# The up projection of a gated feed-forward layer, turned from channels on the partitions to positions on the partitions, with the transpose moved behind it

## The chip, the core and the metric

The kernel is one program on one core of a Trainium2 chip. The metric is the device time of one execution in microseconds (us). TensorE is called PE below, its weight loads PEld, VectorE DVE, ScalarE ACT, GpSimd POOL and SyncE SP. A matmul on PE has a stationary operand of 128 x 128 elements, which a load brings into the array, and a moving operand whose columns stream past it.

## The reference, cut to what matters

One layer: a token mixer with a convolution branch and a state-space branch, cross-attention, and then the feed-forward part, which is all that the change touches. There are 256 positions, a model width of 2048 and a hidden width of 5632. All arrays are 32-bit floats.

```
def causal_dwconv(x, w):
    """Depthwise causal conv over positions. x (B, L, C), w (K, C); output t reads t-K+1..t."""
    ...

def conv_ffn(h, w_up, dw_w, w_down):
    up = causal_dwconv(h @ w_up, dw_w)
    gate, val = jnp.split(up, 2, axis=-1)
    return (jax.nn.silu(gate) * val) @ w_down

h = rmsnorm(x, ffn_norm_g[i])
x = x + conv_ffn(h, ffn_w_up[i], ffn_dw_w[i], ffn_w_down[i])
```

So `h @ w_up` is 256 x 2048 times 2048 x 11264, the convolution has three taps along the positions (FFN_K = 3), with its own three weights for each of the 11264 channels, and the first half of the channels gates the second.

## The kernel before, in words

**Weights and slots.** All weights of the program form one stream of pieces of 128 x 1024 elements, and one piece is one *slot* of work. There are 586 slots. A DMA brings two pieces at once (`raw`, 1 MB, L207). For each piece ACT rounds the values to the matmul's 32-bit format (`hi`, L221) and DVE subtracts that from the original (`lo`, L222), so that a product is made of three terms, hi times hi, lo times hi and hi times lo. `take` asks for the pieces up to three slots ahead (`AHEAD = 3`), and four buffers each hold `hi` and `lo`. So the conversion of the piece for slot n + 3 waits until PE is done with the piece of slot n - 1.

**Two forms of a slot.** `by_token` says which of two forms a block of 512 weight columns has. Both make the same three products, on 6144 moving columns in a slot.

- The *wide* form (`mm_wide`, L250 and L253): the weights are stationary and the activations move. The result has the channels on the partitions. For each 128 x 128 tile of weights there is one matmul with 512 moving columns (the high and the low part of the activations side by side, L250), and one with 256 (L253): 8 and 8 in a slot, 16 weight loads. The results of the high and the low part stand in two halves of PSUM and are added afterwards (L277 on ACT, L278 on DVE).
- The *token* form (`tok_piece`, L300, L301, L304): the activations are stationary and the weights move, 512 columns at a time. The result has the positions on the partitions. There are 12 matmuls and 12 loads in a slot, and all three products add up in one place.

The up projection is wide. The projections before and after it that add to the residual (`w_out`, `xa_w_o`, `ffn_w_down`, and `conv_w_pw`) have the token form.

**The feed-forward stage.** `PAIRS` splits the hidden width into 11 pairs of blocks: a pair is block q of the gates (s = 0) and block 11 + q of the values (s = 1), each of 512 columns and of 8 slots. Pass 1 runs six pairs (96 slots), then the down projection over their 3072 rows (48 slots). Pass 2 runs five pairs (80 slots), then the last part of the down projection (40 slots). After each up block comes the scaling by the root mean square of its position (`rs`, a row that is the same on all partitions, L398 on DVE, into `up`, which has two columns of zeros in front), then the three taps: the first by ACT (L1226), the other two by DVE (L1208), each shifted by one position along the free axis. After block s = 1 of a pair comes the gate: Silu on ACT (L1232), the product on DVE (L1212) and the split into hi and lo for the down projection (L338, L339, into `as` or `fs`).

**Order.** Nothing is scheduled by a planner; the code's own order stands in each engine's queue. `defer(k, fn)` lays work aside until k slots later, and `pump`, at the end of each slot, lets out what is due. So the names below "end of slot k" count slots of the next block. Each engine works through its queue in order.

**Turning.** `turned` (L309) transposes a block of 256 positions x 512 channels on PE: 8 matmuls of 128 x 128 against the unit matrix (L316), into two buffers of PSUM (`aux`, four of them). It is used already where the residual becomes the next projection's activations (`resid`, and `merge` in the mixer). `rows` (L1155) turns the reciprocal root `rc`, which has the positions on the partitions, into the row `rs` by two small matmuls (L1164).

Of the kernel before, what the change touches and what calls it, by code (L numbers as in the profile page):

```python
# [8 lines left out]
F32 = mybir.dt.float32  # L9
F32R = mybir.dt.float32r  # L10
AF = mybir.ActivationFunctionType
ALU = mybir.AluOpType
# [36 lines left out]

BOTH = ((0, 0), (1, 0), (0, 1), (1, 1), (2, 0), (3, 0), (2, 1), (3, 1))  # L50
START = ((0, 0), (0, 1), (1, 0), (1, 1), (2, 0), (3, 0), (2, 1), (3, 1))
FIRST = {("w_in", 4), ("xa_w_kv", 0), ("xa_w_q", 0), ("ffn_w_up", 0)}


def by_token(w, nb):

    return w in ("ssm_w_glu", "conv_w_pw", "w_out", "xa_w_o", "ffn_w_down") or (w, nb // 4) == ("xa_w_kv", 1) or (w == "w_in" and nb > 5)


def stream():  # L60


    o = []

    def g(w, blocks, kqs):
        for nb in blocks:
            if by_token(w, nb):
                o.extend((False, w, 512 * nb, 512 * kq + 256 * h) for kq in kqs for h in range(2))
            elif (w, nb) in FIRST:
                o.extend((True, w, 512 * nb + 256 * h, 512 * kq) for kq, h in (START if w == "w_in" else BOTH))  # L70
            else:
                o.extend((True, w, 512 * nb + 256 * h, 512 * kq) for h in range(2) for kq in kqs)
    k4, k2 = range(4), range(2)
    g("w_in", (4, 5, 2, 0, 3, 1, *range(6, 14)), k4)
    g("xa_w_kv", range(8), k4)
    for b in range(4):
        g("ssm_w_glu", (4 + b, b), k2)
    g("conv_w_pw", range(4), k2)
    g("w_out", range(4), k4)
    g("xa_w_q", range(4), k4)  # L80
    g("xa_w_o", (0, 1), range(3))
    g("xa_w_o", (0, 1), (3,))
    g("xa_w_o", (2, 3), k4)
    for pairs in PAIRS:
        for q in pairs:
            g("ffn_w_up", (q, 11 + q), k4)
        g("ffn_w_down", range(4), pairs)
    assert len(o) % 2 == 0
    return o


class Body:
# [167 lines left out]
    def gemm(self, w, nb, xs, then, kqs=None, after=None):  # L260


        if by_token(w, nb):
            ps = self.mm_tile()
            for n, kq in enumerate(kqs or range(len(xs))):
                self.tok_piece(ps, w, nb, kq, xs[n], n == 0, n == len(xs) - 1)
                if after is not None:
                    after(n)
            self.defer(0, lambda: then(ps))
            return  # L270
# [11 lines left out]
        ps = [None, None]  # L282
        for m, (kq, h) in enumerate((START if w == "w_in" else BOTH) if (w, nb) in FIRST else [(kq, h) for h in range(2) for kq in range(4)]):
            if kq == 0:
# [18 lines left out]
                m = slice(mt * 128, mt * 128 + 128)  # L303
                nc.tensor.matmul(ps[:, mt, :], xh[:, kt, m], wl, start=False, stop=z)  # L304

    def turned(self, x, k, then):


        nc = self.nc  # L309

        def f():
            ps = [self.aux() for _ in range(2)]
            for j in range(4):
                for tt in range(2):
                    o = (j % 2) * 256 + tt * 128
                    nc.tensor.transpose(ps[j // 2][:, o:o + 128], x[:, tt, 128 * j:128 * j + 128], self.ident)  # L316

            def g():
                for j in range(2):
                    then(ps[j].rearrange("p (a t) -> p a t", a=2), j)  # L320
            self.defer(1, g)
        self.defer(k, f)


# [720 lines left out]
    def attend(self, A, xs, rq):  # L1045
        nc = self.nc
        v = nc.vector
# [93 lines left out]
        w = "xa_w_o"  # L1141
        pss = {}

        def outp(b, kq):
            if kq == 0:
                pss[b] = self.mm_tile()
            self.tok_piece(pss[b], w, b, kq, os_[kq], kq == 0, kq == 3)
            if kq == 3:
                self.defer(0, lambda: done(b, pss[b]))

        sq = self.xb.tile([128, 2, 4], F32, tag="sq", name=self.nm("sq"), bufs=2)
        rs, rc = self.rs_tile(), self.xb.tile([128, 2], F32, name="rc3")
        xs2 = [None] * 4

        def rows():  # L1155

            dg = self.st([128, 2, 128])
            for tt in range(2):
                v.tensor_scalar(dg[:, tt, :], self.ident, rc[:, tt:tt + 1], None, ALU.mult)

            def f():
                ps = self.aux()
                for tt in range(2):
                    nc.tensor.matmul(ps[:, tt * 128:tt * 128 + 128], self.ones, dg[:, tt, :], start=True, stop=True)  # L1164
                self.defer(1, lambda: nc.scalar.copy(rs, ps[:, 0:256]))
            self.defer(1, f)

        def done(b, ps):
            x = self.res[:, :, 512 * b:512 * b + 512]
            v.tensor_add(x, ps, x)  # L1170
            self.spare -= 1.2
            xs2[b] = self.split_tiles(self.xb, "b", b)
            self.resid(b, "ffn_g", sq, xs2[b])
            if b == 3:
                self.defer(2, lambda: self.tok_rs(sq, rc))
                self.defer(3, rows)

        def nxt(h):
            def f(n):
# [12 lines left out]
        for b in (2, 3):  # L1192
            for k in range(4):
                outp(b, k)
        return xs2, rs


    def ffn(self, F, xs, rs):
        nc = self.nc
        v = nc.vector  # L1200
        buf = [F.tile([128, 4, 258], F32, name=f"up{a}") for a in range(2)]
        for t in buf:
            nc.gpsimd.memset(t[:, :, 0:2], 0.0)

        def taps(c, u, s, q, ks):
            for k in ks:
                for tap in (1, 2):
                    v.scalar_tensor_tensor(out=c[:, k, :], in0=u[:, k, tap:tap + 256], scalar=self.par("fdw", (44 * s + 4 * q + k) * 3 + tap),  # L1208
                                           in1=c[:, k, :], op0=ALU.mult, op1=ALU.add)

        def gate(cv, hl):
            v.tensor_mul(cv[1], cv[0], cv[1])  # L1212
            self.plain_split(cv[1], *hl)

        sq = self.xb.tile([128, 2, 4], F32, tag="sq", name=self.nm("sq"), bufs=2)
        for pairs in PAIRS:
            act = [None] * len(pairs)
            for n, q in enumerate(pairs):
                cv = []

                def up(ps, s=0, n=n, q=q, cv=cv):
                    u = buf[s]
                    self.scaled(u[:, :, 2:258], ps, rs)
                    c = self.xc() if s else F.tile([128, 4, 256], F32, tag="cv", name=self.nm("cv"), bufs=2)
                    for k in range(4):
                        nc.scalar.activation(c[:, k, :], u[:, k, 0:256], AF.Copy, scale=self.par("fdw", (44 * s + 4 * q + k) * 3))  # L1226
                    self.defer(1, lambda: taps(c, u, s, q, (0, 1)), 1.6)
                    self.defer(2, lambda: taps(c, u, s, q, (2, 3)), 1.6)
                    cv.append(c)
                    if s:  # L1230
                        hl = act[n] = self.split_tiles(self.xa, "a", n) if n < 4 else self.split_tiles(F, "f", n)
                        self.defer(3, lambda: nc.scalar.activation(cv[0], cv[0], AF.Silu))  # L1232
                        self.defer(4, lambda: gate(cv, hl), 1.2)

                for s in range(2):
                    self.gemm("ffn_w_up", 11 * s + q, xs, lambda t, s=s, up=up: up(t, s))
            last = pairs[-1] == 10
            if last:
                gf = self.xb.tile([128, 2048], F32, tag="b0", name="gf", bufs=1)
                nc.sync.dma_start(out=gf, in_=self.i["fg"].partition_broadcast(128))  # L1240
            for b in range(3 if last else 4):
                def down(ps, b=b):
                    x = self.res[:, :, 512 * b:512 * b + 512]
                    v.tensor_add(x, ps, x)
                    self.spare -= 1.2
                    if last:
                        self.resid(b, None, sq, None)
                        self.defer(2, lambda: v.tensor_mul(x, x, gf[:, 512 * b:512 * b + 512].unsqueeze(1).to_broadcast([128, 2, 512])), 1.1)
                self.gemm("ffn_w_down", b, act, down, list(pairs))
        self.finish(sq, gf, act, list(PAIRS[1]))  # L1250
# [160 lines left out]
```

## Time and profile before

| | |
|---|---|
| median of 3 runs | 1709.28 us (1708.51 to 1709.82) |
| the profiled execution | 1709.71 us, its span 1707.9 us |
| PE busy | 1691.1 us, 99% of the span |
| PEld, DVE, ACT busy | 84%, 72%, 52% |
| granted PE clock, mean | 0.998 |
| up projection, pass 1 | 964.48 to 1235.77 us |
| down projection, pass 1 | 1235.77 to 1366.33 us |
| up projection, pass 2 | 1366.33 to 1591.33 us |

The stages' bounds are the starts of their first matmuls. A row of a group of instructions reads: line, engine, operation, output <- inputs, shapes, count, then busy us and the mean ns of one, then idle time before it and what ended it. A row of the chain of waits reads: start us, duration us, what. A matmul's duration holds its pipelined end too, so the time that one costs is read from one start to the next, not from its duration.

### The profile page before, as it was taken

The numbers are of one execution on the slowest core, as the hardware profiler recorded it, in microseconds if no ns is written. First come the engines' busy times: TensorE is split into PE (matmuls) and PEld (weight loads), VectorE is DVE, ScalarE is ACT, GpSimd is POOL, SyncE is SP. The second block draws the span as 40 slices with busy tenths as digits, with TensorE's granted clock in tenths as the row PEclk, the third lists the DMA queues.
The fourth block names the chain that finished last, engine by engine and source line by source line (L and its number), as shares of the span: only waits on it lengthen the run. The fifth ranks groups of instructions, "written<-read, shape, count | busy, mean of one in ns | idle before, by whom it ended". The sixth has DMA issues, their size and how long they took to land.

```text
span 1707.9 us, 22702 instructions
## 1 busy us (share of the span) xinstructions
PE 1691.1 (99%) x8868; PEld 1438.1 (84%) x8868; DVE 1231.5 (72%) x1627; ACT 895.6 (52%) x1200; POOL 4.3 (0%) x14
## 2 busy tenths in 40 slices
PE   7999999999999999999999999999999999999998
PEld 6888888888888888888988888888888888888886
DVE  6879999899999766556565567777764467777754
ACT  6565665765545644455454555554543345555543
POOL 0000000000000000000000000000000000000000
PEclk9999999999999999999999999999999999999999
DMA  7745555765566565655544544555555555555653
GB/s 284 248 178 179 204 203 196 259 237 196 187 231 218 196 255 209 222 186 209 197 161 172 187 171 186 198 197 181 189 197 197 190 182 183 186 179 191 225 195 122
DMA packets 61643, 340.85 MB, mean 200 GB/s; under 512 B 7904, under 2 KB 16224, under 8 KB 24160
## 3 DMA queue, kind: packets, MB, share of 16 engines
q1 hardware_dynamic: 61536, 339.41, 55.7%
q8 instruction: 69, 1.13, 0.3%
q14 instruction: 38, 0.31, 0.1%
HBM read 326.66 MB, written 12.58 MB: 199 GB/s over the span
## 4 chain that ended last, share of the span: by engine, by line
PE 98%; DMA 1%; DVE 0%; ACT 0%; issue 0%; SPq 0%; DVEq 0%; ACTq 0%
PE mm L250 31%; PE mm L253 16%; PE mm L300 15%; PE mm L301 15%; PE mm L304 15%; DMA raw<-in_ws_dram 1%; PE aux L316 1%; PE aux L1263 1%; PE aux L1262 1%; PE aux L1261 1%; PE aux L638 1%; PE aux L685 0%; PE aux L584 0%; PE aux L1083 0%; PE aux L1082 0%; PE aux L1081 0%
## 5 line engine op out<-in xcount | busy, mean ns | idle before, releaser
L222 DVE TENSOR_TENSOR lo<-raw,hi 128x1024 fp32r<-128x1024 f32 (+1 forms) x586 | 708.7, 1218 | 428.3 <-ACT hi L221 427.9
L221 ACT CAST hi<-raw 128x1024 fp32r<-128x1024 f32 (+1 forms) x586 | 608.4, 1048 | 657.0 <-PE mm L301 335.9
L250 PE MATMUL mm<-bs,hi 128*128 128x512 f32 x1664 | 522.7, 395 | 0.0
L253 PEld LDWEIGHTS mm<-bs,lo 128*128 128x128 f32 x1664 | 312.3, 188 | 75.9
L300 PE MATMUL mm<-hi,as 128*128 128x512 f32 x864 | 338.6, 392 | 0.0
L301 PE MATMUL mm<-hi,as 128*128 128x512 f32 x864 | 336.4, 389 | 0.0
L253 PE MATMUL mm<-bs,lo 128*128 128x256 f32 x1664 | 331.6, 281 | 0.0
L304 PE MATMUL mm<-lo,as 128*128 128x512 f32 x864 | 266.2, 389 | 0.0
L250 PEld LDWEIGHTS mm<-bs,hi 128*128 128x128 f32 x1664 | 256.2, 188 | 0.2
L250 PE MATMUL mm<-as,hi 128*128 128x512 f32 x640 | 203.3, 399 | 8.3 <-ACT hi L221 7.5
L300 PEld LDWEIGHTS mm<-hi,as 128*128 128x128 f32 x864 | 162.2, 188 | 34.1 <-issue 0.7
L304 PEld LDWEIGHTS mm<-lo,as 128*128 128x128 f32 x864 | 162.2, 188 | 34.0
L301 PEld LDWEIGHTS mm<-hi,as 128*128 128x128 f32 x864 | 162.3, 188 | 32.7
L253 PEld LDWEIGHTS mm<-as,lo 128*128 128x128 f32 x640 | 120.5, 189 | 30.4 <-DVE lo L222 2.3
L253 PE MATMUL mm<-as,lo 128*128 128x256 f32 x640 | 126.6, 279 | 1.0 <-DVE lo L222 1.0
L250 PEld LDWEIGHTS mm<-as,hi 128*128 128x128 f32 x640 | 98.0, 190 | 9.7 <-ACT hi L221 7.8
L751 DVE SCALAR_TENSOR_TENSOR co<-h,prm,co 128x256 f32<-128x256 f32 x240 | 100.9, 478 | 0.0
L278 DVE TENSOR_TENSOR st<-mm,st 128x512 f32<-128x512 f32 x72 | 49.2, 684 | 9.0 <-ACT st L277 9.0
L300 PE MATMUL mm<-hi,gs 128*128 128x512 f32 x128 | 50.7, 396 | 0.0
L301 PE MATMUL mm<-hi,gs 128*128 128x512 f32 x128 | 50.7, 396 | 0.0
L277 ACT COPY st<-mm 128x512 f32<-128x512 f32 x72 | 41.6, 578 | 0.1
L1208 DVE SCALAR_TENSOR_TENSOR xc<-up,prm,xc 128x256 f32<-128x256 f32 x88 | 40.6, 482 | 1.6
(281 smaller groups left out, 1295.9 us busy)
## 6 DMA issues: line engine op xcount, KB each, us to landing
raw<-in_ws_dram SPq DMA_DIRECT2D x291, 1024.0 KB, 4.8
gd<-st SPq DMA_DIRECT2D x8, 512.0 KB, 6.4
st<-gd SPq DMA_DIRECT2D x8, 512.0 KB, 5.7
xc<-in_mem_dram SPq DMA_DIRECT2D x4, 512.0 KB, 7.2
kd<-st SPq DMA_DIRECT2D x4, 512.0 KB, 4.3
vd<-st SPq DMA_DIRECT2D x4, 512.0 KB, 7.0
res<-in_xt_dram SPq DMA_DIRECT2D x4, 512.0 KB, 5.8
xc<-kd SPq DMA_DIRECT2D x4, 512.0 KB, 5.7
```

What stands on the lines that cost most here:

```text
L221: nc.scalar.copy(hi[:, k], src[:, k])
L222: nc.vector.tensor_sub(lo[:, k], src[:, k], hi[:, k].bitcast(F32))
L250: nc.tensor.matmul(ps[:, ct, :], hi[:, kt, ct * 128:ct * 128 + 128], x.t[:, :, kt, :], start=a, stop=False, skip_group_check=True)
L253: nc.tensor.matmul(ps[:, ct, 0:256], lo[:, kt, ct * 128:ct * 128 + 128], x[0][:, kt, :], start=False, stop=z, skip_group_check=True)
L277: self.nc.scalar.copy(o, ps[:, :, 256:512])
L278: self.nc.vector.tensor_add(o, ps[:, :, 0:256], o)
L300: nc.tensor.matmul(ps[:, mt, :], xh[:, kt, m], wh, start=a, stop=False)
L301: nc.tensor.matmul(ps[:, mt, :], xl[:, kt, m], wh, start=False, stop=False)
L304: nc.tensor.matmul(ps[:, mt, :], xh[:, kt, m], wl, start=False, stop=z)
L316: nc.tensor.transpose(ps[j // 2][:, o:o + 128], x[:, tt, 128 * j:128 * j + 128], self.ident)
L751: v.scalar_tensor_tensor(out=o, in0=self.h[:, k, j:j + 256], scalar=w, in1=o, op0=ALU.mult, op1=ALU.add)
L1208: v.scalar_tensor_tensor(out=c[:, k, :], in0=u[:, k, tap:tap + 256], scalar=self.par("fdw", (44 * s + 4 * q + k) * 3 + tap), in1=c[:, k, : ...
```

## The change

`ffn_w_up` goes into the token form. Its result now stands in one PSUM tile with the positions on the partitions, where the scaling is one number for each partition: ACT scales it out of PSUM into `u` by `rc` (two instructions, L1198 of the changed kernel). `turned` transposes `u` on PE one slot later. The taps read the transposed block where it lies, in PSUM: ACT makes the tap of the same position for two channel tiles (L1204), DVE adds the other two (L1209), now with outputs that start one or two positions later in place of the zero columns. A new argument of `turned`, `apart`, lets out the second half of the block one slot after the first. The gate comes after five slots in place of four. The buffers `up`, their clearing, `rows` and the row `rs` of this stage fall away, and so do the addition of the two PSUM halves and the interleaved order of the first up block (`FIRST`).

```
-FIRST = {("w_in", 4), ("xa_w_kv", 0), ("xa_w_q", 0), ("ffn_w_up", 0)}
+FIRST = {("w_in", 4), ("xa_w_kv", 0), ("xa_w_q", 0)}
...
-    return w in ("ssm_w_glu", "conv_w_pw", "w_out", "xa_w_o", "ffn_w_down") or ...
-    return w in ("ssm_w_glu", "conv_w_pw", "w_out", "xa_w_o", "ffn_w_down") or (w, nb // 4) == ("xa_w_kv", 1) or (w == "w_in" and nb > 5)
+    return w in ("ssm_w_glu", "conv_w_pw", "w_out", "xa_w_o", "ffn_w_up", "ffn_w_down") or (w, nb // 4) == ("xa_w_kv", 1) or (w == "w_in" and nb > 5)
...
-    def turned(self, x, k, then):
+    def turned(self, x, k, then, apart=0):
...
-            def g():
-                for j in range(2):
-                    then(ps[j].rearrange("p (a t) -> p a t", a=2), j)
-            self.defer(1, g)
+            for j in range(2):
+                self.defer(1 + j * apart, lambda j=j: then(ps[j].rearrange("p (a t) -> p a t", a=2), j))
         self.defer(k, f)
...
-        def rows():
-            dg = self.st([128, 2, 128])
...
-                self.defer(3, rows)
...
-        return xs2, rs
+        return xs2, rc
...
-    def ffn(self, F, xs, rs):
+    def ffn(self, F, xs, rc):
...
                 def up(ps, s=0, n=n, q=q, cv=cv):
-                    u = buf[s]
-                    self.scaled(u[:, :, 2:258], ps, rs)
+                    u = F.tile([128, 2, 512], F32, tag="u", name=self.nm("u"), bufs=2)
+                    for tt in range(2):
+                        nc.scalar.activation(u[:, tt, :], ps[:, tt, :], AF.Copy, scale=rc[:, tt:tt + 1])
                     c = self.xc() if s else F.tile([128, 4, 256], F32, tag="cv", name=self.nm("cv"), bufs=2)
-                    for k in range(4):
-                        nc.scalar.activation(c[:, k, :], u[:, k, 0:256], AF.Copy, scale=self.par("fdw", (44 * s + 4 * q + k) * 3))
-                    self.defer(1, lambda: taps(c, u, s, q, (0, 1)), 1.6)
-                    self.defer(2, lambda: taps(c, u, s, q, (2, 3)), 1.6)
+
+                    def taps(p, j):
+                        w = lambda k, tap: self.par("fdw", (44 * s + 4 * q + k) * 3 + tap)
+                        for a in range(2):
+                            nc.scalar.activation(c[:, 2 * j + a, :], p[:, a, :], AF.Copy, scale=w(2 * j + a, 2))
+                        for a in range(2):
+                            k = 2 * j + a
+                            for tap in (1, 0):
+                                d = 2 - tap
+                                v.scalar_tensor_tensor(out=c[:, k, d:256], in0=p[:, a, 0:256 - d], scalar=w(k, tap), in1=c[:, k, d:256],
+                                                       op0=ALU.mult, op1=ALU.add)
+                        self.spare -= 1.9
+                    self.turned(u, 1, taps, 1)
                     cv.append(c)
...
-                        self.defer(4, lambda: gate(cv, hl), 1.2)
+                        self.defer(5, lambda: gate(cv, hl), 1.2)
```

On PE, in the first up block before the change (`mm_8209` and `mm_8267` are its two halves, `bs` the activations, `aux_8344` the row `rs`):

```order
L253 MATMUL mm_8209<-bs_8058,lo_8235 128x256 x2
L1164 MATMUL aux_8344<-st_8321,cst 128x128 x2
L250 MATMUL mm_8209<-bs_8231,hi_8268 128x512 x2
L253 MATMUL mm_8209<-bs_8231,lo_8269 128x256 x2
...
L250 MATMUL mm_8267<-bs_8058,hi_8301 128x512 x2
L253 MATMUL mm_8267<-bs_8058,lo_8302 128x256 x2
```

And on PE after the change, between the second and the third slot of the second up block (`mm_8367`), where the first block's `u_8384` is turned into two buffers of PSUM:

```order
L301 MATMUL mm_8367<-hi_8333,bs_7839 128x512
L304 MATMUL mm_8367<-lo_8334,bs_7839 128x512 x2
L316 MATMUL aux_8406<-cst,u_8384 128x128 x4
L316 MATMUL aux_8407<-cst,u_8384 128x128 x4
L300 MATMUL mm_8367<-hi_8351,bs_7897 128x512
L301 MATMUL mm_8367<-hi_8351,bs_7897 128x512
```

The small matmuls of the row are gone, the slots have changed their form, and 8 transposes stand behind the second slot of each following block.

On ACT, from the end of the first up block on, before the change (`st_8390` takes the low half of the first block out of PSUM, `cv_8439` is its tap):

```order
L277 COPY st_8390<-mm_8209 128x512
L221 CAST hi_8395<-raw_8299 128x1024
L221 CAST hi_8416<-raw_8299 128x1024
L277 COPY st_8390<-mm_8267 128x512
L1226 ACTIVATE cv_8439<-up_8204,prm 128x256 x4
L221 CAST hi_8446<-raw_8347 128x1024
L221 CAST hi_8470<-raw_8347 128x1024
```

And after it:

```order
L221 CAST hi_8368<-raw_8281 128x1024
L1198 ACTIVATE u_8384<-mm_8204,rc_6502 128x512 x2
L221 CAST hi_8390<-raw_8315 128x1024
L221 CAST hi_8416<-raw_8315 128x1024
L1204 ACTIVATE cv_8387<-aux_8406,prm 128x256 x2
L221 CAST hi_8440<-raw_8349 128x1024
L1204 ACTIVATE cv_8387<-aux_8407,prm 128x256 x2
```

The two copies out of PSUM have become two scalings, one behind the other, and the four first taps come two and three slots later, two at a time, each behind the conversion of a weight piece.

More of the change, by code (lines that the diff above doesn't have):

```diff
@@ L1151, in attend @@
         sq = self.xb.tile([128, 2, 4], F32, tag="sq", name=self.nm("sq"), bufs=2)
-        rs, rc = self.rs_tile(), self.xb.tile([128, 2], F32, name="rc3")
+        rc = self.xb.tile([128, 2], F32, name="rc3")
         xs2 = [None] * 4
-        def rows():
-            dg = self.st([128, 2, 128])
[L1158 to L1166, printed above, removed]
         def done(b, ps):
@@ L1194, in attend @@
                 outp(b, k)
-        return xs2, rs
-    def ffn(self, F, xs, rs):
+        return xs2, rc
+    def ffn(self, F, xs, rc):
         nc = self.nc
         v = nc.vector
[L1201 to L1209, printed above, removed]
         def gate(cv, hl):
```

## The prediction

> **What bounds the kernel now.** I read the page first: span, busy shares, granted clock, and the chain of work that ended last.
>
> ```profile
> span 1707.9 us, 22702 instructions
> PE 1691.1 (99%) x8868; PEld 1438.1 (84%) x8868; DVE 1231.5 (72%) x1627; ACT 895.6 (52%) x1200; POOL 4.3 (0%) x14
> PEclk9999999999999999999999999999999999999999
> PE 98%; DMA 1%; DVE 0%; ACT 0%; issue 0%; SPq 0%; DVEq 0%; ACTq 0%
> ```
>
> The chain is PE from end to end. A busy row alone would not prove that, since a matmul's row holds its pipelined end, so next I read who made PE wait, in the whole program:
>
> ```profile
> PE mm L250 <- ACT hi L221: 7.5, 2, 6.4
> PE mm L253 <- DVE lo L222: 1.0, 2, 0.5
> PE mm L250 <- DVE as L333: 0.7, 1, 0.7
> ```
>
> That is 9.2 us, in the mixer's first stage by the operands' names (`as` from x). In the feed-forward stage PE waits for nobody. So the time of that stage is the sum of the intervals between PE's starts, and what ACT and DVE win is worth nothing as long as they stay ahead. The question is therefore how many us of PE the change takes away and adds. I take that from the stages, by the timeline of PE at their bounds and the busy time of each engine in the windows between them (window, length, then PE, PEld, DVE, ACT, POOL, clock, DMA share, GB/s):
>
> ```profile
> 964.48 0.63 PE L250 MATMUL mm<-bs,hi 128*128 128x512 f32 x2
> ...
> 1235.77 0.39 PE L300 MATMUL mm<-hi,as 128*128 128x512 f32 x1
> ...
> 1366.33 0.63 PE L250 MATMUL mm<-bs,hi 128*128 128x512 f32 x2
> ...
> 1591.33 0.39 PE L300 MATMUL mm<-hi,as 128*128 128x512 f32 x1
> ```
>
> ```profile
> 1366.33:1591.33 225.00, 225.00 (x1282) 195.87 (x1281) 158.75 (x189) 113.46 (x144) 0.00 (x0) 1.00 0.52 187
> 1235.77:1366.33 130.56, 130.56 (x578) 108.15 (x577) 69.37 (x63) 54.51 (x56) 0.00 (x0) 1.00 0.54 193
> 964.48:1235.77 271.29, 271.29 (x1549) 236.33 (x1548) 194.00 (x237) 142.57 (x186) 0.00 (x0) 1.00 0.52 187
> 696.00:742.00 46.00, 46.00 (x212) 38.26 (x212) 25.32 (x27) 22.54 (x34) 0.00 (x0) 1.00 0.58 211
> ```
>
> Pass 2 of the up projection is 80 wide slots in 225.00 us: 2.8125 us each, 22.50 us a block. The down projection of pass 1 is 48 token slots with nothing else on PE in 130.56 us: 2.72 us each. DVE is busy 15.9 us and ACT 11.3 us of a block's 22.5.
>
> **The change, part by part.**
>
> *The slots' form.* 22 blocks of 8 slots go from 22.50 to 8 x 2.72 = 21.76 us: 0.74 us saved in each, 16.3 us in all. Each slot has the same 6144 moving columns, so this is no less arithmetic, but 12 matmuls in place of 16.
>
> *The transposes.* Each block brings 8 of them (L316), and they stand in PE's own queue. The chain of waits shows the same sets at work in the token stages of today, as their starts:
>
> ```profile
> 639.13 0.87 PE aux L316 x8
> 650.91 0.87 PE aux L316 x8
> ...
> 697.13 0.87 PE aux L316 x8
> 719.79 0.87 PE aux L316 x8
> 742.45 0.87 PE aux L316 x8
> ...
> 970.29 0.87 PE aux L316 x8
> ```
>
> In `w_out` the sets are 22.66 us apart, twice, with 8 token slots between two starts: 22.66 - 21.76 = 0.90 us a set. In `conv_w_pw` they are 11.78 us apart with 4 slots: 11.78 - 10.88 = 0.90 again. It is a little more than the 0.87 of the row, since the next matmul starts late too. 22 sets make 19.8 us. An up block after the change is just what a `w_out` block is now, 8 token slots and one set, so I expect it at 22.66 us against 22.50: +0.16 us in each.
>
> *The row `rs`.* Its two small matmuls fall away:
>
> ```profile
> 979.24 0.40 PE L253 MATMUL mm<-bs,lo 128*128 128x256 f32 x2
> 979.48 0.60 PE L1164 MATMUL aux<-st,cst 128*128 128x128 f32 x4
> ...
> 980.38 0.39 PE L253 MATMUL mm<-bs,lo 128*128 128x256 f32 x2
> ```
>
> From one L253 pair to the next are 1.14 us, against 2.8125 / 4 = 0.70 elsewhere: 0.43 us saved, once. The set that is in the first up block already (970.29) goes from between wide slots to between token slots: pass 1 without the row and at 22.50 a block leaves 271.29 - 0.43 - 270.00 = 0.86 for it, so +0.04.
>
> *ACT and DVE.* The rows by group, with forms kept apart, price the work that changes hands:
>
> ```profile
> L962 ACT ACTIVATE st<-mm,rcm 128x512 f32<-128x512 f32 x8 | 5.0, 680 | 0.0
> L277 ACT COPY st<-mm 128x512 f32<-128x512 f32 x72 | 41.6, 578 | 0.1
> L1226 ACT ACTIVATE cv<-up,prm 128x256 f32<-128x256 f32 x44 | 18.8, 498 | 29.4 <-DVE up L398 29.4
> L1033 ACT ACTIVATE bs<-aux,prm 128x256 fp32r<-128x256 f32 x32 | 12.5, 471 | 0.0
> L278 DVE TENSOR_TENSOR st<-mm,st 128x512 f32<-128x512 f32 x72 | 49.2, 684 | 9.0 <-ACT st L277 9.0
> L398 DVE TENSOR_TENSOR up<-st,rs 128x1024 f32<-128x1024 f32 x22 | 26.9, 1225 | 0.8
> L1208 DVE SCALAR_TENSOR_TENSOR cv<-up,prm,cv 128x256 f32<-128x256 f32 x88 | 40.6, 482 | 1.6
> L1035 DVE SCALAR_TENSOR_TENSOR bs<-aux,prm,bs 128x256 fp32r<-128x256 f32 x32 | 13.2, 476 | 0.9 <-ACT bs L1033 0.9
> ```
>
> Per block ACT gives up 2 copies (L277) and 4 taps (L1226), and gets 2 scalings out of PSUM by a number for each partition (L962 is that form) and 4 taps out of PSUM (L1033): 2 x 680 + 4 x 471 - 2 x 578 - 4 x 498 ns = +0.1 us. DVE gives up two additions and the scaling, 2 x 684 + 1225 = 2.6 us, and keeps 8 taps, which cost 476 ns out of PSUM (L1035) against 482. So DVE falls to about 13.3 us of a block and ACT stays near 11.4. As neither bounds the stage, the 2.6 us are worth nothing. What hides all this is the 22.66 us of PE in a block; if PE stood still, all of it would come out.
>
> *The new waits.* PE now waits in its own queue for `u`, and behind that wait stand all following matmuls. Today's evacuation after the last up block, and the way to the last gate, show how late these can be (ACT, then DVE):
>
> ```profile
> 1591.28 1.05 ACT L221 CAST hi<-raw 128x1024 fp32r<-128x1024 f32 x1 [1.77 <-PE mm L250]
> 1592.24 0.58 ACT L277 COPY st<-mm 128x512 f32<-128x512 f32 x1
> ```
>
> ```profile
> 1604.12 2.35 DVE L222 TENSOR_TENSOR lo<-raw,hi 128x1024 fp32r<-128x1024 f32 x2
> 1606.39 1.22 DVE L1212 TENSOR_TENSOR xc<-cv,xc 128x1024 f32<-128x1024 f32 x1
> 1608.72 1.22 DVE L339 TENSOR_TENSOR fs<-xc,fs 128x1024 fp32r<-128x1024 f32 x1 [1.11 <-ACT fs L338]
> ```
>
> The copy out of PSUM starts 0.9 us after the block's end (1591.33), so `u` is done 0.9 + 2 x 0.68 = 2.3 us after it. The transposes stand behind two slots, at 5.44 us. PE does not wait: 3.1 us to spare. The four PSUM buffers of `turned` are needed again only 8 slots later. The weight pieces that ACT converts behind `u` and the taps have the same queue ahead of them as today, within 0.1 us, so they are costed at nothing.
>
> *The gate, one slot later.* Its product of the last pair of pass 2 is read by the down projection's ninth slot: today at 1591.33 + 8 x 2.72 = 1613.09, and it is complete at 1609.94. Put a slot later (+2.72), and with the set of transposes ahead of both, 0.43 us remain: the pessimistic bound. The other bound is the DVE queue: the product stood behind two conversions (1604.12) in a queue which will be 2.6 us a block shorter, so it could come as much earlier, 3 us to spare. I take no wait. In pass 1 the last pair is read two slots later still.
>
> *SP, DMA, POOL.* The same 1 MB pieces in the same order; two clearings of POOL fall away beside other work. Nothing.
>
> **The sum:** -16.3 + 19.8 - 0.43 + 0.04 = +3.1 us on the profiled execution's 1709.71 us, so 1712.8 us. That execution lies 0.43 us above the median of the runs, 1709.28 us; against the median the forecast is **1712.4 us**, +0.18%. A measurement of this kernel can tell about 0.2% (3.4 us) from no change, so this is "no change" by a hair. The intervals are read to 0.01 us; an error of 0.01 us in a block's price makes 0.2 us in the sum, and between chip runs the medians spread by about 0.5 us. So +2.2 to +4.2 us is the forecast's own range: 1711.5 to 1713.5 us.
>
> [...] In the window from 696 to 742 us, with the sets at 697.13 and 719.79 in it, the clock granted to PE is 1.00, and in the windows without transposes it is 1.00 too. [...]
>
> **The rivals.**
>
> 1. *The last gate is late* (slower). ACT's cast of the product waits for DVE, behind it stand ACT's next conversions, and PE's ninth down slot of pass 2 reads the result. For it: the pessimistic bound above is only 0.43 us. Against it: the shorter DVE queue. It decides as soon as PE stands still for 0.3 us, since the forecast is already that close to the limit. Late by one slot it costs 2.7 us: +5.8, 1715.1 us.
> 2. *PE waits at the transposes or for conversions in each block* (slower). For it: one late `u` holds all that is behind it. Against it: 3.1 us to spare, and `w_out` runs this pattern at 22.66. Half a us a block costs 11 us more than the forecast: 1723.4 us.
> 3. *A transpose costs less* (faster). Small matmuls with 64-row weights run closer in the state-space branch:
>
> ```profile
> 498.44 1.02 PE aux L685 x16
> ```
>
>    That is 0.064 us each, so 0.51 a set in place of 0.90: 22 x 0.39 = 8.6 us less, 1703.8 us, faster by 0.3%. Against it: the instructions are the very L316 of `turned`, and all three spacings above give 0.90.
> 4. *The clock falls behind each set.* If the slot behind a set took as long again, 22 x 2.72 = 60 us: 1772 us. Against it: the clock rows.
>
> That the change does not do what it says can be left out: the transposes stand in PE's order at 22 places, and no wide matmul of the stage is left.
>
> **How the numbers follow.** Forecast 0.80, rival 1 0.07, rival 2 0.06, rival 3 0.05, rival 4 0.02. Of the forecast's 0.80, the limit of +3.4 us lies half a spread above its middle, so I give 0.55 to "within 0.2%" and 0.25 to slower. Slower in all: 0.25 + 0.07 + 0.06 + 0.02 = 0.40; faster 0.05. The range goes from 1710 us (a set at 0.80 in place of 0.90 us, 2.2 us less) to 1717 us (rival 1 with a margin, or 0.2 us a block of rival 2); outside are rivals 3 and 4 and most of rival 2, and some 0.06 for what I did not see.
>
> **What would show it.** Right: in the profile after, sets of L316 in the up stage 22.66 us apart; up blocks of 22.66 us in the windows; no row of PE waiting for ACT or DVE in the stage; DVE near 13 us a block. The forecast falls if the sets are not 0.90 us, if token slots with `bs` as stationary operand are not 2.72 us, or if PE's waits name `u` or the gate's `as` or `fs`.

## The result, and the profile after

The changed kernel takes 1727.41 us (median; 1727.01 to 1727.95) against 1709.47 us before: 17.9 us more, ratio 1.0105, 95% interval 1.0093 to 1.0117. The forecast was 1712.4 us, in a range from 1710 to 1717 us. The measured time lies above that range, and the change is slower by about 1% where "within 0.2%" was the likeliest outcome. All ratios here compare runs at a granted clock of at least 0.997; one run of the kernel before, 1855.61 us at a clock of 0.85, is left out of them.

The page after, its span, busy row and chain:

```profile
span 1725.8 us, 21538 instructions
PE 1711.0 (99%) x8336; PEld 1425.2 (83%) x8336; DVE 1184.1 (69%) x1559; ACT 900.3 (52%) x1199; POOL 4.2 (0%) x12
PE 99%; DMA 0%; DVE 0%; SPq 0%; issue 0%; ACT 0%; DVEq 0%
```

Who made PE wait after the change, in the whole program:

```profile
PE mm L250 <- ACT hi L221: 6.6, 1, 6.6
PE mm L250 <- DVE as L331: 0.6, 1, 0.6
```

Both waits are in the mixer's first stage, as before, and none is in the feed-forward stage. So rivals 1 and 2 did not happen, and the chain is PE from end to end as before: the 17.9 us are longer work on PE. The windows by stage (up of pass 1, down of pass 1, up of pass 2) say where:

```profile
964.25:1243.93 279.68, 279.68 (x1250) 226.92 (x1249) 169.38 (x201) 144.73 (x184) 0.00 (x0) 1.00 0.50 181
1243.93:1375.82 131.89, 131.89 (x586) 108.98 (x584) 67.88 (x61) 54.97 (x57) 0.00 (x0) 1.00 0.53 191
1375.82:1608.03 232.21, 232.21 (x1033) 188.25 (x1032) 138.88 (x161) 115.40 (x143) 0.00 (x0) 1.00 0.51 181
```

The up stages grew from 271.29 to 279.68 and from 225.00 to 232.21 us, the down stage between them from 130.56 to 131.89, by 1.3 us, of which 0.9 is a set of transposes that now stands in it. DVE fell to 138.88 / 10 = 13.9 us a block. The granted clock is 1.00 with up to twelve sets of transposes in a window, so rival 4 falls here; but a set is 0.87 us among some 22 us of matmuls, and no run has a long stretch of transposes alone.

The chain's rows of the sets in the up stage:

```profile
993.35 0.87 PE aux L316 x8
1016.64 0.87 PE aux L316 x8
1039.95 0.87 PE aux L316 x8
```

A set is as long as forecast, 0.87, but the sets are 23.30 us apart and not 22.66. Less 0.90 for the set, 22.40 us are left for 8 slots: 2.80 us a slot, not 2.72. The timeline of PE shows it in the steady flow, from one L300 to the first L300 of the next group of six matmuls:

```profile
1002.48 0.40 PE L300 MATMUL mm<-hi,bs 128*128 128x512 f32 x1
...
1003.89 0.39 PE L300 MATMUL mm<-hi,bs 128*128 128x512 f32 x1
```

1.41 us for six where the down projection takes 1.36. Over a whole slot each matmul comes 2.80 / 12 = 0.233 us after the last, and not 2.72 / 12 = 0.227. The groups of PE, kept apart by operand, show the same in the mean ns of one (last number before the second bar). In these rows `hi` is the moving tile of weights, and the tile behind it (`bs`, `as`, `fs` or `gs`) is the stationary one. After the change:

```profile
L301 PE MATMUL mm<-hi,bs 128*128 128x512 f32 x704 | 278.2, 395 | 0.0
L301 PE MATMUL mm<-hi,as 128*128 128x512 f32 x864 | 336.5, 389 | 0.0
L301 PE MATMUL mm<-hi,fs 128*128 128x512 f32 x88 | 34.6, 393 | 0.0
L301 PE MATMUL mm<-hi,gs 128*128 128x512 f32 x128 | 50.7, 396 | 0.0
```

and before it:

```profile
L301 PE MATMUL mm<-hi,as 128*128 128x512 f32 x864 | 336.4, 389 | 0.0
L301 PE MATMUL mm<-hi,fs 128*128 128x512 f32 x88 | 34.2, 389 | 0.0
L301 PE MATMUL mm<-hi,gs 128*128 128x512 f32 x128 | 50.7, 396 | 0.0
```

The same instruction, the same shape, the same clock, and two speeds: 389 with `as` as the stationary operand, 395 with `bs`, 396 with `gs`. And `fs` changed from 389 to 393, though its instructions are the same in both kernels.

### The profile page after: what moved, and what is told of

Same layout as the page of the kernel before. It is cut to its first block, busy times and chain, and to the rows that moved or that the text cites. A ratio compares the mean times of both kernels' runs of the same rounds, so it can differ in the third digit from the quotient of the medians.

```text
span 1725.8 us, 21538 instructions
## 1 busy us (share of the span) xinstructions
PE 1711.0 (99%) x8336; PEld 1425.2 (83%) x8336; DVE 1184.1 (69%) x1559; ACT 900.3 (52%) x1199; POOL 4.2 (0%) x12
## 4 chain that ended last, share of the span: by engine, by line
PE 99%; DMA 0%; DVE 0%; SPq 0%; issue 0%; ACT 0%; DVEq 0%
PE mm L300 25%; PE mm L304 25%; PE mm L301 25%; PE mm L250 12%; PE mm L253 6%; PE aux L316 2%; PE aux L1246 1%; PE aux L1247 1%; PE aux L1245 1%; PE aux L636 1%; PE aux L683 0%; PE aux L582 0%; DMA raw<-in_ws_dram 0%; PE aux L1081 0%; PE aux L1080 0%; PE aux L1079 0%
## 5 line engine op out<-in xcount | busy, mean ns | idle before, releaser
L300 PE MATMUL mm<-hi,as 128*128 128x512 f32 x864 | 338.8, 392 | 0.0
L301 PE MATMUL mm<-hi,as 128*128 128x512 f32 x864 | 336.5, 389 | 0.0
L300 PE MATMUL mm<-hi,bs 128*128 128x512 f32 x704 | 280.3, 398 | 0.0
L301 PE MATMUL mm<-hi,bs 128*128 128x512 f32 x704 | 278.2, 395 | 0.0
L304 PE MATMUL mm<-lo,bs 128*128 128x512 f32 x704 | 221.9, 396 | 0.0
L300 PEld LDWEIGHTS mm<-hi,as 128*128 128x128 f32 x864 | 162.2, 188 | 34.2 <-issue 0.7
L301 PEld LDWEIGHTS mm<-hi,as 128*128 128x128 f32 x864 | 162.3, 188 | 32.8
L304 PEld LDWEIGHTS mm<-lo,bs 128*128 128x128 f32 x704 | 132.7, 188 | 31.6
L300 PEld LDWEIGHTS mm<-hi,bs 128*128 128x128 f32 x704 | 132.6, 188 | 31.3
L301 PEld LDWEIGHTS mm<-hi,bs 128*128 128x128 f32 x704 | 132.6, 188 | 31.0
L250 PE MATMUL mm<-bs,hi 128*128 128x512 f32 x256 | 80.8, 396 | 0.0
L253 PEld LDWEIGHTS mm<-bs,lo 128*128 128x128 f32 x256 | 48.0, 188 | 11.8
L253 PE MATMUL mm<-bs,lo 128*128 128x256 f32 x256 | 50.8, 279 | 0.0
```

Source lines behind the costliest of these rows:

```text
L250: nc.tensor.matmul(ps[:, ct, :], hi[:, kt, ct * 128:ct * 128 + 128], x.t[:, :, kt, :], start=a, stop=False, skip_group_check=True)
L253: nc.tensor.matmul(ps[:, ct, 0:256], lo[:, kt, ct * 128:ct * 128 + 128], x[0][:, kt, :], start=False, stop=z, skip_group_check=True)
L300: nc.tensor.matmul(ps[:, mt, :], xh[:, kt, m], wh, start=a, stop=False)
L301: nc.tensor.matmul(ps[:, mt, :], xl[:, kt, m], wh, start=False, stop=False)
```

## The experiments

One thing that differs between these tiles is where they lie in SBUF, the memory in which this kernel keeps the operands of these matmuls. In the built programs `hi`, `lo`, `as` and `ch` (the convolution's branch) all start at remainder 160 when their address in a partition is divided by 256 bytes. Call the remainder of an activation tile's start less that of `hi` and `lo`, again by 256, its distance. It is 96, 96, 96 and 128 bytes for `b` tiles 0 to 3, which make up `bs`, and 128 and 160 for the two `gs` tiles. The two `fs` tiles had 0 before and have 192 after, because the buffers in front of them changed their size. A tile at distance 0 is called aligned below. The theory (A) is that it sets the spacing of the matmuls. The rivals are the values in the tiles (B), and the traffic of ACT, DVE and DMA in the stage (C). All kernels below are complete ones; a gap is an unused tile that moves what comes behind it, and gaps further on put all other tiles back to their old remainder. Runs of one kernel spread by up to 2.4 us (1711.56 to 1713.99 in the first experiment), so where a kernel ran once, only differences well above that are read from its time.

**Aligned b tiles, in the changed kernel** (11 runs):

```
+GAPS = (160, 0, 0, 224)
...
+                    if GAPS[b]:
+                        P2.tile([128, GAPS[b] // 4], F32, name=f"gap{b}")
                     xs[b] = self.split_tiles(P2, "b", b)
```

> The changed kernel, with unused gaps in SBUF (160 bytes ahead of the first b tile, 224 ahead of the last) so that all four b tiles, the stationary operands of the up projection, start at the same remainder by 256 bytes as the weight tiles hi and lo (160); every other tile keeps its remainder. Theory A (the place of the stationary tile in SBUF sets the spacing of the matmuls): up slots fall from 2.80 to 2.72 us, blocks from 23.31 to 22.66 us, 22 x 0.65 = 14 us less, and some 0.5 us in the query projection: 1712 to 1713 us. Theory B (the values in the b tiles, through power or otherwise): nothing changes, 1727.4 us. Theory C (ACT, DVE and DMA traffic of the up stage disturbs PE's reads): nothing changes, 1727.4 us.

Measured: 1712.9 us, 1.002 of the kernel before (1.0011 to 1.0029), its profiled execution 1711.56 us. Windows of the two up stages, the group on `bs` (its line is one further down), and two sets of the chain:

```profile
962.52:1234.45 271.93, 271.93 (x1250) 226.22 (x1248) 169.36 (x201) 144.49 (x184) 0.00 (x0) 1.00 0.52 186
...
1366.33:1592.03 225.70, 225.70 (x1033) 187.69 (x1032) 138.86 (x161) 115.16 (x143) 0.00 (x0) 1.00 0.52 186
```

```profile
L302 PE MATMUL mm<-hi,bs 128*128 128x512 f32 x704 | 274.0, 389 | 0.0
```

```profile
1036.12 0.87 PE aux L317 x8
1058.78 0.87 PE aux L317 x8
```

The blocks are 22.66 us, to the hundredth. Gaps of 384 bytes in each partition ahead of the tiles, and 128 behind them, give back 14.5 us. B and C, which foresaw no change, are out for this effect: values and traffic are the same.

**Aligned b tiles, in the kernel before** (7 runs; the same edit there):

> The kernel before, with the same gaps, so that the b tiles (here the moving operand of the up and query projections) start at the remainder 160 as hi and lo do. Theory A: the wide group of four matmuls falls from 0.703 us to the 0.697 us that it takes where the moving operand lies at remainder 160 (the mixer's input projection): 4 x 0.006 x (176 + 32) slots = 5 us less, about 1704.5 us. Theories B and C: 1709.4 us.

Measured: 1704.32 us, 0.9969 (0.9957 to 0.998). The window of pass 2:

```profile
1362.36:1585.28 222.92, 222.92 (x1281) 194.50 (x1280) 158.77 (x189) 113.36 (x144) 0.00 (x0) 1.00 0.53 189
```

The wide block goes from 22.50 to 22.29 us. The wide form, in which `bs` moves and the weights are stationary, paid too, but a third of what the token form pays: 0.026 us a slot against 0.08.

**hi and lo moved instead** (one run): a gap of 96 bytes ahead of `hi`, which gives `hi` and `lo` the remainder of b tiles 0 to 2 and puts all `as` tiles at distance 160.

```
+            if s == 0:
+                self.wp.tile([128, 24], F32, name="gapw")
             hi, lo = (self.wp.tile([128, 1024], F32R, tag=t, name=self.nm(t), bufs=self.AHEAD + 1) for t in ("hi", "lo"))
```

> The changed kernel with hi and lo moved by 96 bytes, to the remainder 0 that the b tiles 0 to 2 have, all activation tiles at their old remainders. Theory A in the form that the distance between the two operands counts: up slots on b tiles 0 to 2 fall to 2.72 us, and the slots of the other token projections, on as tiles, rise from 2.72 to about 2.80 us; with 250 or so of these and 80 wide ones, in all about 1730 to 1740 us. Theory A in the form that the stationary tile's own remainder counts: up slots stay at 2.80, the others at 2.72, 1727 us. Theories B and C: 1727 us.

Measured: 1738.3 us. The groups, and the timeline in `w_out`:

```profile
L304 PE MATMUL mm<-hi,as 128*128 128x512 f32 x864 | 340.6, 394 | 0.0
...
L304 PE MATMUL mm<-hi,bs 128*128 128x512 f32 x704 | 274.9, 391 | 0.0
```

```profile
700.65 0.39 PE L303 MATMUL mm<-hi,as 128*128 128x512 f32 x1
...
702.05 0.39 PE L303 MATMUL mm<-hi,as 128*128 128x512 f32 x1
```

No activation tile has moved against the 256 bytes, and the roles are exchanged: `w_out` takes 1.40 us a group where it took 1.36, and up groups on b tiles 0 to 2 are at 1.36 (the 391 is the mean with tile 3, still 32 off, at 1.40). So it is the distance between the operands, not the place of the stationary one alone, and not the traffic of a stage or the values in a tile: the stages and the values are the same, and fast and slow have changed places.

**Two sweeps of the distance** (one run each): other gaps ahead of the four b tiles, in the changed kernel. They put tiles 0 to 3 at 0, 32, 64 and 160 bytes, and at 192, 224, 96 and 128.

> The changed kernel with the b tiles at four distances from hi and lo by the remainder of 256 bytes: 0, 32, 64, 160 for b tiles 0, 1, 2, 3 (96, 96, 96, 128 before). Two slots of each block use each tile. Theory A: the slots on b tile 0 take 2.72 us, that on tile 3 about 2.80, and 1 and 2 tell how the spacing follows the distance; the block lies between 22.66 and 23.31 us. Theories B and C: all slots stay at 2.80 us.

> The changed kernel with b tiles 0 to 3 at distances 192, 224, 96 and 128 by the remainder of 256 bytes. Theory A: slots on tiles 2 and 3 as in the changed kernel (96: 1.405, 128: 1.394 us for six matmuls); 192 near the 1.374 that the fs tiles show at that distance; 224 is open, 1.36 to 1.41. In all 1719 to 1728 us. A tile's own name or contents having a say (theory B) would keep tiles 0 to 2 at 1.405.

Measured: 1723.1 and 1724.4 us. In the first, PE's timeline of a group on tile 0 (distance 0) and, one set of transposes later, of a group on tile 1 (32):

```profile
1012.25 0.39 PE L301 MATMUL mm<-hi,bs 128*128 128x512 f32 x1
...
1013.61 0.39 PE L301 MATMUL mm<-hi,bs 128*128 128x512 f32 x1
...
1017.25 0.40 PE L301 MATMUL mm<-hi,bs 128*128 128x512 f32 x1
...
1018.65 0.40 PE L301 MATMUL mm<-hi,bs 128*128 128x512 f32 x1
```

That is 1.36 us and 1.40 us in one block. In the second, PE's timeline where the block's last tile (distance 128) gives way to the next block's first (192):

```profile
1031.93 0.40 PE L301 MATMUL mm<-hi,bs 128*128 128x512 f32 x1
...
1033.33 0.39 PE L301 MATMUL mm<-hi,bs 128*128 128x512 f32 x1
...
1034.70 0.39 PE L301 MATMUL mm<-hi,bs 128*128 128x512 f32 x1
```

1.40 us for the last group on tile 3, 1.37 for the first on tile 0. The medians of the groups of six, tile by tile, worked out from the starts of the first matmuls (up to 88 groups each) over all these runs:

| distance, bytes | 0 | 32 | 64 | 96 | 128 | 160 | 192 | 224 |
|---|---|---|---|---|---|---|---|---|
| us for six matmuls | 1.360 | 1.400 | 1.400 | 1.402 to 1.407 | 1.395 to 1.400 | 1.400 | 1.373 | 1.400 |

Of these distances only 0 is fast (1.360); 192 is a third of the way up (1.373), and all others are at about 1.40. A distance of 256 bytes is as good as 0: in the run with aligned b tiles, tiles 0 to 2 lie 256 bytes off `hi` by the remainder of 512 and tile 3 lies 0 off, and the groups of all four have a median of 1.360 us. Tile 0 of the first sweep, at distance 0 between blocks that end at distance 160, had a median of 1.370 and not 1.360; no run shows why.

**lo alone moved** (one run): `hi` aligned with all b and `as` tiles, `lo` 96 bytes further on, which puts these tiles at distance 160 from `lo`.

> The changed kernel with aligned b tiles, in which the lo tiles alone lie 96 bytes further, off all activation tiles by 96 of the remainder, while hi stays aligned with them. If the distance counts between the two operands of one matmul: the four matmuls on hi in a group of six keep 0.227 us, the two on lo (L304 and its like) take 0.234, the group 1.36 + 2 x 0.0075 = 1.375 us, and the token slots of the whole program lose 0.03 us each: 474 x 0.03 = 14 us, 1727 us. If one operand off its place slows the whole group: 1.405 us and 474 x 0.09 = 43 us, 1756 us. If the activation tile's neighbour hi decides: no change, 1712.9 us.

Measured: 1740.7 us, between the expectations of 1727 and 1756 us. The groups of the matmuls on `hi` (second in the pair) and on `lo`:

```profile
L306 PE MATMUL mm<-hi,as 128*128 128x512 f32 x864 | 338.3, 392 | 0.0
...
L309 PE MATMUL mm<-lo,as 128*128 128x512 f32 x864 | 272.2, 396 | 0.0
```

Both are slower than 389, and the groups of six on `as` take 1.393 us in the median. From one start to the next, the medians are 231, 231, 236 and 228 ns behind the four matmuls on `hi` and 236 and 232 ns behind the two on `lo`; with all of them aligned (the first experiment) each is 227 ns. So more than half of the 33 ns that a group loses falls behind matmuls whose own operands are aligned. The cost is not kept to the matmul whose operands are off, and two of six lose most of what all six would (1.400 us). My picture of each matmul paying for its own operands was wrong.

**The transposes twice** (one run): aligned b tiles, and each set issued a second time over the first.

```
-            for j in range(4):
+            for j in (range(4) if not apart else (0, 1, 2, 3, 0, 1, 2, 3)):
```

> The changed kernel with aligned b tiles, in which each of the 22 sets of transposes of u is issued twice, the second over the first. If the transposes stand on PE's path at their full price (the prediction's term of 0.90 us a set): 22 x 0.87 to 0.90 = 19 to 20 us more than 1712.9 us, about 1732.4 us, the blocks at about 23.55 us. If part of a set's price were its place between two slots (the switch from matmuls to transposes and back) the second pass costs less, 0.70 us or so, 1728 us. If they were hidden beside other work: no change.

Measured: 1731.8 us. The chain:

```profile
1015.38 1.75 PE aux L317 x16
1038.91 1.75 PE aux L317 x16
```

Blocks of 23.53 us, 0.87 more than 22.66. A set lies on the path with all of its time; nothing of it is hidden, and rival 3 falls too.

**All aligned** (11 runs and 5): the changed kernel with `gs` and `fs` aligned as well, and the kernel before with `gs` aligned as well (its `fs` tiles were).

> The changed kernel with b, gs and the two fs tiles all aligned. Theory A: 2.6 us for gs and some 0.6 us for fs below 1712.9 us, about 1709.7 us; so with all operands aligned the change itself costs about 8 us against the kernel before with the same alignment, being 22 blocks of 22.66 in place of 22.30 us. If the alignment had been all that the change was slow by, the two would end within 0.2%.

> The kernel before with the b tiles aligned to hi and lo by the remainder of 256 bytes as in the run before, and the two gs tiles too (128 and 160 bytes off until now), the stationary operands of the 32 token slots of the state-space branch's GLU projection. Theory A, by distance: these slots fall from 2.80 to 2.72 us, 32 x 0.08 = 2.6 us below the kernel with aligned b tiles alone: about 1701.7 us. Theory B (values): no further change, 1704.3 us.

Measured: 1709.36 us for the changed kernel, ratio 1.0 to the kernel before as it was (0.9991 to 1.0009), and 1701.49 us for the kernel before, 0.9955 (0.9942 to 0.9968). Pass 2 of the first and of the second:

```profile
1365.29:1590.99 225.70, 225.70 (x1033) 187.64 (x1032) 138.86 (x161) 115.14 (x143) 0.00 (x0) 1.00 0.53 186
```

```profile
1360.67:1583.60 222.93, 222.93 (x1282) 194.51 (x1281) 158.74 (x189) 113.39 (x144) 0.00 (x0) 1.00 0.53 189
```

With both in their best place the change costs 1709.36 - 1701.49 = 7.9 us, close to 22 x (22.66 - 22.29) = 8.1 us less the 0.4 us of the row `rs`. The kernel before with gaps beats both kernels of the comparison.

## Why the prediction was wrong, and where it was right

**The step that failed** is *the slots' form*: "22 blocks of 8 slots go from 22.50 to 8 x 2.72 = 21.76 us". The 2.72 us were measured on `as` tiles, and I carried them to `bs` tiles as if the form alone set the price. On `bs` the slot takes 2.80 us: 22 x 8 x 0.08 = 14.1 us more than in the sum. That leaves 17.9 - 3.1 - 14.1 = 0.7 us, and the `fs` tiles that the change shifted make most of it: 88 matmuls of L301 on `fs` are 44 groups of six, at 1.373 in place of 1.360 us, 0.6 us. The sum had no term for them.

The same slip stands in *an up block after the change is just what a `w_out` block is now*. It is, in instructions; not in where they read from. And the profile of before held the counter-example: the `gs` rows, 396 against 389, token slots with nothing but other tiles. Costed by them a slot is 2.80 us, and the sum comes to 1712.4 + 14.1 = 1726.5 us, 0.9 below what was measured. I took the row nearest in name and did not ask why another stage with the same instruction differed, so the upper end of the range was missing. The prediction's last sentence does name "token slots with `bs` as stationary operand" that "are not 2.72 us" as a sign of being wrong, but no rival and no price stood behind it.

**Right:** the transposes (0.87 in the chain, 0.90 by their spacing), shown at full price by doubling them; the two small matmuls; DVE's relief being worth nothing (13.9 us a block, 13.3 forecast); no wait at `u`, at the taps or at the gate; the clock. With the b tiles aligned the sum's terms come out: blocks of 22.66 us, 1712.9 us against 1712.4 us forecast. That the total is so close has a little luck in it: the 0.6 us of `fs` are in it, and against them the query projection, still wide, won 0.4 us by the same gaps (from its first matmul to its last, 106.0 us became 105.6). Against a kernel before that is aligned too it would have been 7.9 us more and not 3.1, since the 22.50 us held the wide form's own loss of 0.21 us a block.

**Rivals:** none of the four happened. The change did what it says: 22 sets, no wait, and no wide matmul left in the up stages.

## What to carry to other kernels

In this kernel a matmul's price read in one stage held in another only where its operands lay alike (389 ns on `as` and 395 on `bs`, and 389 on both with the b tiles aligned). So compare the same instruction over all stages first, and if two groups of one shape have different means, find out why before one of them goes into a sum. In a kernel bound by PE, look at where the stationary and the moving tiles start: in this one an equal remainder by 256 bytes cost a few hundred unused bytes in each partition and was worth 0.45% of the kernel before, as much as the whole rewrite costs where both are aligned. A change of a buffer's size moves the tiles behind it, so a kernel can change its pace in places that the diff does not touch, as it did on `fs` (389 to 393 ns).

## What the runs showed of the hardware

- Operand starts that differed by 32, 64, 96, 128, 160 or 224 bytes, by the remainder of 256, made a steady flow of 128 x 128 by 512 matmuls in the 32-bit format take about 0.233 us each (1.395 to 1.407 us for six), where it took 0.227 (1.360) at a difference of 0; at 192 bytes it was 0.229 (1.373). With weights as the stationary operand and 512 and 256 columns in turn, four matmuls took 0.703 us at distances of 96 and 128 and 0.697 us at 0 (80 slots of 16 matmuls in 225.00 and 222.92 us).
- The fastest steady flow of these matmuls timed here took 227 ns for each, at a granted clock of 1.00, with a load for each matmul (8336 of both in the changed kernel).
- Two matmuls in six with `lo` 96 bytes further on made all six take 1.393 us in place of 1.360 (0.232 us each in the mean), and more than half of the loss fell behind the other four. Why the distance matters, and by which path the loss spreads, stays open: the runs show it by the operands' places and by nothing else, and no run separates the weight load's read from the moving operand's.
